# A mixture of softmaxes on one core: stores placed earlier in ScalarE's order, a buffer wait moved to ScalarE, an earlier prior, and a coarser last load

## The chip, the cores and the metric

One NeuronCore of a Trainium2 chip runs the kernel. The metric is the device time of one execution in microseconds (us); medians of several runs are quoted. The profile's span, from the first to the last instruction, is about 1.8 us shorter than the time.

## The reference

```python
prior_probs = softmax(prior, axis=-1)            # [32, 128, 4]
softmax     = softmax(logits, axis=-1)           # [32, 128, 4, 4096], fp32
mixture     = np.sum(prior_probs[..., None] * softmax, axis=2)   # [32, 128, 4096]
```

268.4 MB of logits are read once and 67.1 MB of result written once. Each row (b, s) has four heads of 4096 logits.

## The kernel before

The 4096 rows are cut into 32 units (U) of 128 rows. A unit is loaded to one of two buffers (8.4 MB). ScalarE takes four exponentials with their sums, VectorE takes the reciprocals of the sums, GpSimd multiplies them by the prior, and VectorE adds the four weighted heads into one of two output buffers, which is then stored (2.1 MB).

```python
def load(u):
    if u == 0 or u >= U - 3:
        cuts = (0, 2, 3, 4) if u == U - 1 else (0, 2, 4)
    else:
        cuts = (0, H)
    for h, to in zip(cuts, cuts[1:]):
        ld = nc.sync.dma_start(out=ltile[:, u % 2, h:to], in_=lg[u // J, u % J, :, h:to, :])
        if u >= 2:
            only(ld, adds[u - 2, 0] if h == 0 else exps[u - 2, to - 1])   # all it waits for
        ...
# for each unit u:
free = (stores[u - 2],) if bufd and u >= 2 else ()     # output buffer is free again
m = H if u < U - 4 else 2                              # heads per coefficient step
for h in range(H):
    late = h == H - 1 and 4 <= u < U - 3
    if h == H - 1 and 0 < u < U - 3:
        store(u - 1, obuf[:, (u - 1) % 2], nc.scalar)  # on ScalarE's queue, waits for the last add of u-1
    exp(h, *((stores[u - 4],) if late else ()))
    if (h + 1) % m: continue
    g = h + 1 - m
    mul = weigh(g, m, *(free if g == 0 else ()))       # VectorE reciprocal, then GpSimd product
    for k in range(g, h + 1):
        n = 2 if u == U - 1 and k == H - 1 else 1      # last add of all: two halves,
        for c in range(n):                             # each stored as it is ready
            add(k, mul, c * V // n, (c + 1) * V // n)
            ...
if u + 2 < U: load(u + 2)
# stores of units 28 to 31 are issued on SP's queue, behind the loads
```

A small function that runs at the end of the build moves the very first load ahead of the opening barrier.

The softmax here doesn't subtract the row's maximum and nothing guards it: scores larger than these inputs give would overflow.

## Time and profile before

| | before |
|---|---|
| time, median | 780.93 us |
| span | 779.3 us |
| VectorE, ScalarE busy | 67%, 60% |
| DMA rate over the span | 431 GB/s |

The page also follows the chain of work that ended last. It gives the share of the span by what the chain passed through:

```profile
DMA 64%; ACT 27%; DVE 6%; issue 2%; POOL 0%; DVEq 0%; POOLq 0%
```

For the kernel before it runs mostly through loads.

### The profile page before, as it was taken

The numbers are of one execution on the slowest core, as the hardware profiler recorded it, in microseconds if no ns is written. First come the engines' busy times: TensorE is split into PE (matmuls) and PEld (weight loads), VectorE is DVE, ScalarE is ACT, GpSimd is POOL, SyncE is SP. The second block draws the span as 40 slices with busy tenths as digits, with TensorE's granted clock in tenths as the row PEclk, the third lists the DMA queues.
The fourth block names the chain that finished last, engine by engine and source line by source line (L and its number), as shares of the span: only waits on it lengthen the run. The fifth ranks groups of instructions, "written<-read, shape, count | busy, mean of one in ns | idle before, by whom it ended". The sixth has DMA issues, their size and how long they took to land.

```text
span 779.3 us, 654 instructions
## 1 busy us (share of the span) xinstructions
DVE 521.0 (67%) x174; ACT 466.7 (60%) x258; POOL 8.3 (1%) x41
## 2 busy tenths in 40 slices
DVE  4447875558755587555775557855578655689886
ACT  4476555775457755577555675546765567657782
POOL 0000000000000000000000000000000000000000
DMA  9999999999999999999999999999999999999998
GB/s 407 457 417 401 470 407 434 428 461 428 405 467 403 458 420 433 442 443 418 431 454 407 454 408 467 420 415 447 432 442 417 463 399 463 410 427 433 434 429 377
DMA packets 10117, 335.66 MB, mean 431 GB/s; under 512 B 1136, under 2 KB 1136, under 8 KB 1152
## 3 DMA queue, kind: packets, MB, share of 16 engines
q1 hardware_dynamic: 6048, 276.83, 82.3%
q10 hardware_dynamic: 4064, 58.79, 17.6%
q14 instruction: 5, 0.04, 0.0%
HBM read 268.50 MB, written 67.11 MB: 431 GB/s over the span
## 4 chain that ended last, share of the span: by engine, by line
DMA 64%; ACT 27%; DVE 6%; issue 2%; POOL 0%; DVEq 0%; POOLq 0%
DMA ltile<-in_logits_dram 62%; ACT ebuf L159 19%; ACT ltile L159 8%; DVE obuf L177 5%; DMA out_dram<-obuf 2%; DVE ltile L183 1%; POOL coeff L170 0%; DVE rden L168 0%; DVEq L240 0%; POOLq L240 0%; POOLq L170 0%
## 5 line engine op out<-in xcount | busy, mean ns | idle before, releaser
L183 DVE SCALAR_TENSOR_TENSOR obuf<-ebuf,coeff,obuf 128x4096 f32<-128x4096 f32 x90 | 403.6, 4484 | 3.8 <-POOL coeff L170 0.6
L159 ACT ACTIVATE ebuf<-ltile 128x4096 f32<-128x4096 f32 x90 | 322.9, 3589 | 7.4 <-DMA ltile<-in_logits_dram 7.4
L159 ACT ACTIVATE ltile<-ltile 128x4096 f32<-128x4096 f32 x38 | 137.3, 3614 | 280.6 <-DMA ltile<-in_logits_dram 280.6
L168 DVE RECIPROCAL rden<-dsum 128x4 f32<-128x4 f32 (+1 forms) x36 | 6.3, 175 | 227.9 <-ACT ebuf L159 225.1
L177 DVE TENSOR_SCALAR obuf<-ltile,coeff 128x4096 f32<-128x4096 f32 x30 | 70.6, 2353 | 10.2 <-POOL coeff L170 10.2
L183 DVE SCALAR_TENSOR_TENSOR ltile<-ltile,coeff 128x4096 f32<-128x4096 f32 (+1 forms) x7 | 27.0, 3875 | 0.8 <-POOL coeff L170 0.6
L159 ACT ACTIVATION_READ_ACCUMULATOR ebuf<-ltile 128x1 f32 x90 | 16.8, 186 | 0.0
L170 POOL TENSOR_TENSOR coeff<-rden,pp 128x4 f32<-128x4 f32 (+1 forms) x36 | 7.2, 200 | 755.3 <-DVE rden L168 745.4
L159 ACT ACTIVATION_READ_ACCUMULATOR ltile<-ltile 128x1 f32 x38 | 7.1, 186 | 0.0
L139 DVE TENSOR_REDUCE pmax<-pr 16x256 f32<-16x1024 f32 x1 | 1.2, 1208 | 7.8 <-DMA pr<-in_prior_dram 7.8
L141 ACT ACTIVATE pr<-pr 16x1024 f32<-16x1024 f32 x1 | 1.1, 1055 | 7.8 <-DVE pr L140 7.8
L177 DVE TENSOR_SCALAR ltile<-ltile,coeff 128x4096 f32<-128x4096 f32 x2 | 4.7, 2354 | 0.6 <-POOL coeff L170 0.6
L144 DVE TENSOR_TENSOR pn<-pr,pmax 16x1024 f32<-16x1024 f32 x1 | 1.9, 1939 | 0.1
L141 ACT ACT_TABLE_LOAD x1 | 1.3, 1283 | 1.2 <-PEq L229 1.2
L142 DVE TENSOR_REDUCE pmax<-pr 16x256 f32<-16x1024 f32 x1 | 1.2, 1207 | 1.1 <-ACT pr L141 1.1
L149 DVE STREAM_TRANSPOSE pp<-pn 32x256 f32<-32x256 f32 x4 | 1.7, 435 | 0.1
L143 DVE RECIPROCAL pmax<-pmax 16x256 f32<-16x256 f32 x1 | 1.7, 1741 | 0.0
L140 DVE TENSOR_TENSOR pr<-pr,pmax 16x1024 f32<-16x1024 f32 x1 | 1.2, 1211 | 0.0
L138 POOL MEMSET pn<- 32x1024 f32 x1 | 0.9, 941 | 0.3 <-POOLq L229 0.3
L229 POOL MEMSET const-bfloat16-1.0<- 128x1 bf16 x1 | 0.1, 106 | 0.0
L229 POOL MEMSET const-uint8-127<- 128x1 uint8 x1 | 0.1, 106 | 0.0
L229 POOL MEMSET const-float32-0.0<- 128x1 f32 x1 | 0.1, 103 | 0.2 <-issue 0.2
(1 smaller groups left out, 0.1 us busy)
## 6 DMA issues: line engine op xcount, KB each, us to landing
out_dram<-obuf ACTq DMA_DIRECT2D x28, 2048.0 KB, 29.4
ltile<-in_logits_dram SPq DMA_DIRECT2D x7, 4096.0 KB, 26.1
ltile<-in_logits_dram SPq DMA_DIRECT2D x2, 2048.0 KB, 30.9
out_dram<-obuf SPq DMA_DIRECT2D x2, 2048.0 KB, 33.9
out_dram<-ltile SPq DMA_DIRECT2D x1, 2048.0 KB, 17.2
out_dram<-ltile SPq DMA_DIRECT2D x2, 1024.0 KB, 4.8
ltile<-in_logits_dram SPq DMA_DIRECT2D x28, 30.9
pr<-in_prior_dram ACTq DMA_DIRECT2D x1, 64.0 KB, 7.0
```

What stands on the lines that cost most here:

```text
L139: nc.vector.reduce_max(pmax, pr, axis=AX.X)
L140: nc.vector.tensor_sub(pr, pr, pmax.unsqueeze(2).to_broadcast([G, R, H]))
L141: nc.scalar.activation(pr, pr, AF.Exp)
L142: nc.vector.reduce_sum(pmax, pr, axis=AX.X)
L143: nc.vector.reciprocal(pmax, pmax)
L144: nc.vector.tensor_mul(pn[0:G].rearrange("g h r -> g r h"), pr, pmax.unsqueeze(2).to_broadcast([G, R, H]))
L149: nc.vector.transpose(pp[32 * t : 32 * (t + 1)], pq[:, :, :, 32 * t : 32 * (t + 1)])
L159: ex = nc.scalar.activation(es[h], lt[:, h], AF.Exp, accum_out=dsum[:, u, h : h + 1])
L168: rc = nc.vector.reciprocal(rden[:, u, h : h + n], dsum[:, u, h : h + n])
L170: mul = nc.gpsimd.tensor_mul(coeff[:, u, h : h + n], rden[:, u, h : h + n], ppu[:, h : h + n])
L177: st = nc.vector.tensor_scalar(out=acc[:, lo:hi], in0=es[h][:, lo:hi], scalar1=coeff[:, u, h : h + 1], scalar2=None, op0=ALU.mult,)
L183: st = nc.vector.scalar_tensor_tensor(out=acc[:, lo:hi], in0=es[h][:, lo:hi], scalar=coeff[:, u, h : h + 1], in1=acc[:, lo:hi], op0=ALU.mu ...
```

## The change

The intent, as the change's own words have it: stores ahead of the third exponential (instead of the fourth), the wait for the free output buffer on ScalarE instead of GpSimd, the prior's load also ahead of the opening barrier, and the last unit in two pieces instead of three. The core of the diff:

```diff
-            cuts = (0, 2, 3, 4) if u == U - 1 else (0, 2, 4)
+            cuts = (0, 2, 4)
...
             for h in range(H):
-                late = h == H - 1 and 4 <= u < U - 3
-                if h == H - 1 and 0 < u < U - 3:
+                if h == 2 and 0 < u < U - 3:
                     store(u - 1, obuf[:, (u - 1) % 2], nc.scalar)
-                exp(h, *((stores[u - 4],) if late else ()))
+                exp(h, *(free if m == H and h == H - 1 else ()))
...
-                mul = weigh(g, m, *(free if g == 0 else ()))
+                mul = weigh(g, m, *(free if m < H and g == 0 else ()))
```

The function at the end of the build (cut here) now moves the first DMA of ScalarE, the prior, as well as that of SP.

More of the change, by code (lines that the diff above doesn't have):

```diff
@@ L11, with early_transfers, of @@
 AX = mybir.AxisListType
-def early_first_load(nc):
+def early_transfers(nc):
     blocks = nc.main_func.blocks
-    first = next(
-        (b, i)
-        for b in blocks[1:]
-        for i in b.instructions
-        if i.engine == mybir.EngineType.SP and i.opcode == "DMACopy"
-    )
-    block, ins = first
-    assert not ins.sync_info.on_wait
-    block.instructions.remove(ins)
-    at = next(
-        n
-        for n, i in enumerate(blocks[0].instructions)
-        if i.engine == mybir.EngineType.SP and i.opcode == "Drain"
-    )
-    blocks[0].instructions.insert(at, ins)
+    def of(block, engine, opcode):
+        return next(
+            (i for i in block.instructions if i.engine == engine and i.opcode == opcode), None
+        )
+    for engine in (mybir.EngineType.SP, mybir.EngineType.Activation):
+        body = next(b for b in blocks[1:] if of(b, engine, "DMACopy"))
+        ins = of(body, engine, "DMACopy")
+        assert not ins.sync_info.on_wait
+        body.instructions.remove(ins)
+        drain = of(blocks[0], engine, "Drain")
+        blocks[0].instructions.insert(blocks[0].instructions.index(drain), ins)
 @with_exitstack
@@ L46 @@
     nc = tc.nc
-    nc.at_finalize(early_first_load)
+    nc.at_finalize(early_transfers)
     B, S, H, V = logits.shape
```

## The prediction

> **What bounds the kernel now.** I read the page of the kernel before first, for who is busy:
>
> ```profile
> DVE 521.0 (67%) x174; ACT 466.7 (60%) x258; POOL 8.3 (1%) x41
> ...
> DMA  9999999999999999999999999999999999999998
> ...
> HBM read 268.50 MB, written 67.11 MB: 431 GB/s over the span
> ```
>
> No compute engine is over 67%; the DMA engines are at 90% or more in 39 of 40 slices. A digit of 9 could still hide gaps, so the second view is busy time in stretches (the last two columns are DMA share and GB/s):
>
> ```profile
> 1.00:772.00 771.00, 519.61 (x174) 466.74 (x258) 7.92 (x37) 1.00 1.00 433
> 772.00:777.00 5.00, 1.42 (x1) 0.00 (x0) 0.00 (x0) 1.00 1.00 413
> 777.00:779.30 2.30, 0.00 (x0) 0.00 (x0) 0.00 (x0) 1.00 0.08 32
> ```
>
> From 1.0 to 777 us the sixteen DMA engines are never free. 335.6 MB at 433 GB/s are 775 us of the 779.3. So the middle of the kernel is worth exactly nothing to a change that moves no bytes, unless it starves the queue; only the first microsecond and the last seven can change. The third view is the timeline of one steady unit (start, duration, engine, operation):
>
> ```profile
> 379.04 3.62 ACT L159 ACTIVATE ltile<-ltile 128x4096 f32<-128x4096 f32 x1 [9.67 <-DMA ltile<-in_logits_dram]
> ...
> 385.83 0.34 ACTq L113 DMA_DIRECT2D out_dram<-obuf  x1
> ...
> 386.25 3.56 ACT L159 ACTIVATE ebuf<-ltile 128x4096 f32<-128x4096 f32 x1
> ...
> 389.85 3.60 ACT L159 ACTIVATE ebuf<-ltile 128x4096 f32<-128x4096 f32 x1
> ...
> 396.45 0.33 SPq L100 DMA_DIRECT2D ltile<-in_logits_dram  x1
> 396.46 13.53 DVE L183 SCALAR_TENSOR_TENSOR obuf<-ebuf,coeff,obuf 128x4096 f32<-128x4096 f32 x3
> 403.21 3.62 ACT L159 ACTIVATE ltile<-ltile 128x4096 f32<-128x4096 f32 x1 [9.67 <-DMA ltile<-in_logits_dram]
> ...
> 410.01 0.34 ACTq L113 DMA_DIRECT2D out_dram<-obuf  x1
> ```
>
> A unit starts every 24.17 us (403.21 - 379.04), which is its 10.49 MB at 434 GB/s. ScalarE idles 9.67 us per unit waiting for its load. The load issued at 396.45 (unit 17) cannot begin to move until the one before it (unit 16) has landed, about 402.8, just ahead of its exponential at 403.21: some 6 us of lead. That lead is the number to watch. Last, the end of the timeline, units 30 and 31:
>
> ```profile
> 739.50 3.62 ACT L159 ACTIVATE ltile<-ltile 128x4096 f32<-128x4096 f32 x1 [2.41 <-DMA ltile<-in_logits_dram]
> ...
> 749.22 3.62 ACT L159 ACTIVATE ltile<-ltile 128x4096 f32<-128x4096 f32 x1 [2.41 <-DMA ltile<-in_logits_dram]
> ...
> 756.43 3.60 ACT L159 ACTIVATE ltile<-ltile 128x4096 f32<-128x4096 f32 x1
> ...
> 764.29 9.13 DVE L183 SCALAR_TENSOR_TENSOR ltile<-ltile,coeff 128x4096 f32<-128x4096 f32 x3 [0.31 <-POOL coeff L170]
> ```
>
> The halves of units 30 and 31 arrive 9.72 us apart (739.50 to 749.22). The third exponential of unit 31, at 756.43, shows no wait: its data, cut as a quarter of its own, had come.
>
> **What the Trainium skill says.** (1) "DMA: Bandwidth & Descriptors", section "Where 436 GB/s comes from": sixteen ports give 435.2 GB/s. The trace agrees: 433 to 434 GB/s in full stretches, so the rate has no room left. (2) The same page, "Queues, rings and completion order": each DMA engine takes turns between its queues packet by packet. The trace agrees in kind: a 2 MB store takes 29.4 us (median) to land beside a load, far over the 4.9 us that 2.1 MB take at 434 GB/s, because it shares each turn with the loads' larger rows. (3) "Perfetto Trace Analysis", section "Sequencer Loop": an engine's sequencer takes instructions in order, so what stands behind a waiting DMA issue waits too. The line at 385.83 agrees: the store issues the moment its last add ends (VectorE's run before it ended at 385.8), with the third exponential already handed on.
>
> **The change part by part.**
>
> *Store ahead of the third exponential.* No instruction is added; the order on ScalarE becomes exp, exp, store, exp, exp. The store waits for the last add of the unit before. In the steady state that add ends at 409.99, and the third exponential ran at 410.43 anyway. With the store in front it starts at 410.01 + 0.34 + some hundredths, so about the same. The store itself is issued when the add ends, before and after: nothing gained. It does close a loop: third exponential (386.25) to the end of that unit's adds and the store issue (410.01) is 23.76 us, plus 0.34 for the issue, 24.10 us, plus the dispatch, against a DMA period of 24.17. The loop just fits. In units 2 and 3, whose adds end late (store issues at 72.7 and 95.6), the exponential slips by 1.3 to 1.9 us, and that slip then dies away only slowly.
>
> *Tile wait on ScalarE.* The wait for the store of two units back moves from GpSimd's small product (418.00 in the unit that starts at 403.21) to the fourth exponential (414.02). That store was issued at 385.83; with 29.4 us to landing it is down at 415.2, plus some 0.4 us for the wait to be seen. So the fourth exponential is held for 1.2 to 1.7 us in every unit, where before the wait was over when GpSimd came to it. Slips of the two kinds overlap; they do not add. So the exponentials, the first weighted product and the next load's issue come 1.3 to 2 us later, 26 times. Of the load's lead of 6 us at least 4 remain, and a load needs about 1 us from issue to first bytes (first load: issue at 0.00, DMA busy from 1.0). Cost on the path: 0.
>
> *Prior issued ahead of the opening barrier.* It is issued at about 0.1 instead of 0.79 us. It landed at 7.8; its chain ended with the transposes at 18.2, and the first product that needs it ran at 29.98, after unit 0's last exponential. 0.7 us less of 11.7 us of slack: 0.
>
> *Last unit in two halves.* One of 71 transfers goes, worth about 0 at this rate. But the third exponential must now wait for the whole second half: 749.22 + 9.72 = 758.94 instead of 756.43, so 2.5 us later. The fourth follows at once (it stood at 760.03). The last reciprocal, product and adds all slip by 2.5 us: the last adds start at 766.8 instead of 764.3 and end at 775.9 instead of 773.4.
>
> What of this reaches the end? Ahead of unit 31's stores, the SP queue holds the three stores of units 28 to 30. Behind the last load (landed 758.5, the exponential's wait less some 0.45) they take 3 x 4.86 = 14.6 us, to 773.1 on the latest engines, and unit 31's two half stores 2 x 2.43, to 778.0. Before, the halves were issued at 771.2 and 773.5, in time to queue, so DMA set the end. Now the first half is issued at 773.6 and moves from about 774.5: the engines stand idle for 1.3 to 2.5 us. The second is issued at 775.9, moves from 776.9, is done at 779.3 to 779.4. End: +1.3 to 1.4 us of the 2.5; the rest was queueing.
>
> Sum: 0 + 0 + 0 + 1.35, so 780.93 + 1.35 = 782.3 us.
>
> **The rivals.**
> *A. The loop on ScalarE becomes the bound.* If the dispatch behind the store costs 0.2 us instead of hundredths, the loop is 24.30 us, 0.13 over the DMA period; over 25 units the slip grows by 3.2 us, to about 5, and eats the load's lead. For it: 24.10 against 24.17 is a thin margin. Against: the table load behind the prior's issue followed within 0.03 us (issue 0.79 + 0.39, load at 1.21). It would make 783 to 786 us.
> *B. The end is hidden, or the front gains.* If the second half comes earlier, or the moved prior frees the start, the time stays at 780.5 to 781.2. Against: 9.72 us between halves is steady three times over.
> *C. The whole 2.5 us reach the end*, if the half stores were not queued behind others: 783.4. Against: DMA share 1.00 up to 777 us.
>
> **Range and chances.** Centre 782.3 us. Below, 780.8 is B; above, C and a mild A reach 785. To be 2% off either way takes 15.6 us. A gain of that size is excluded by 775 us of transfers at the ceiling. A loss would need rival A at four times its size. Faster 0.003, same 0.987, slower 0.01.
>
> **What would show it.** In the changed profile: the period of units stays 24.17 us and the DMA share 1.00 up to about 772 us (else A). The fourth exponential waits for a store, 1 to 2 us in most units, and GpSimd no longer does but once or twice near the end. In unit 31 the third exponential waits for its load until about 758.9, the last adds end near 775.9, and a DMA gap of 1 to 2.5 us opens near 773. The span is near 780.7. If the span is 779.3 or less, the step about the last unit was wrong; if the period is over 24.2, the step about the loop was.

## The result, and the profile after

The changed kernel takes 783.14 us (783.01 to 783.27, 6 runs), the kernel before 780.94 us in the same rounds: 2.2 us or 0.28% slower, ratio 1.0028 with a 95% interval of 1.0015 to 1.0041. The span grew by the same 2.2 us, from 779.3 to 781.5.

Busy time by stretches, the changed kernel (the last two columns are DMA share and GB/s):

```profile
1.00:772.00 771.00, 517.12 (x173) 469.89 (x258) 8.13 (x37) 1.00 1.00 433
772.00:777.00 5.00, 3.99 (x2) 0.00 (x0) 0.00 (x0) 1.00 0.53 216
777.00:781.50 4.50, 0.00 (x0) 0.00 (x0) 0.00 (x0) 1.00 0.57 235
```

Up to 772 us the transfers do not differ: 433 GB/s, as before. Then, from 772 to 777 us, the DMA share falls to 0.53, where the kernel before had 1.00 (its line is in the prediction). All but some 0.1 us of the loss arises at the end: unit 31's first exponential starts at 749.34, where it started at 749.22 before.

The end of the timeline shows why (start, duration, engine, line, operation):

```profile
749.34 3.62 ACT L157 ACTIVATE ltile<-ltile 128x4096 f32<-128x4096 f32 x1 [2.41 <-DMA ltile<-in_logits_dram]
...
759.04 3.62 ACT L157 ACTIVATE ltile<-ltile 128x4096 f32<-128x4096 f32 x1 [2.39 <-DMA ltile<-in_logits_dram]
...
766.86 9.14 DVE L181 SCALAR_TENSOR_TENSOR ltile<-ltile,coeff 128x4096 f32<-128x4096 f32 x3 [0.31 <-POOL coeff L168]
773.76 2.60 SPq L111 DMA_DIRECT2D out_dram<-ltile  x2
```

The third exponential of unit 31 now waits 2.39 us for its load, where it ran at 756.43 without a wait. The last adds start at 766.86 instead of 764.29, and the first half store is issued at 773.76. In the kernel before, the same view has the half stores here:

```profile
771.19 2.60 SPq L113 DMA_DIRECT2D out_dram<-ltile  x2
```

The DMA view from 771 to 781.5 us, in 40 slices of 0.26 us (a packet counts in the slice in which it starts, so the first digits are too low), first of the kernel before:

```profile
DMA  4976599999899989899998831100000000000000
```

and of the changed kernel:

```profile
DMA  5911110000000886999977999886999930000000
```

The row of zeros, 772.6 to 774.4 us, is the gap: the queue is empty and the results are still being added. By the packets' own times in the trace, the DMA engines end their earlier stores between 771.8 and 773.16, and the half store starts on them from 774.59.

In the middle, one unit of the changed kernel:

```profile
387.13 0.34 ACTq L111 DMA_DIRECT2D out_dram<-obuf  x1
387.52 3.59 ACT L157 ACTIVATE ebuf<-ltile 128x4096 f32<-128x4096 f32 x1 [1.30 <-DVE obuf L181]
...
411.30 0.34 ACTq L111 DMA_DIRECT2D out_dram<-obuf  x1
411.68 3.59 ACT L157 ACTIVATE ebuf<-ltile 128x4096 f32<-128x4096 f32 x1 [1.29 <-DVE obuf L181]
```

The third exponential now stands behind the store issue and so waits 1.3 us for VectorE's adds. From one third exponential to the next are 24.16 us, the loop that the prediction worked out. The store, though moved ahead in the order, is issued later than before (411.30 against 410.01 us), because the adds that it waits for have slipped too. And the chain that ended last reads:

```profile
DVE 55%; ACT 25%; DMA 15%; issue 2%; ACTq 1%; POOL 1%; DVEq 0%; SPq 0%; POOLq 0%
```

Taken alone this line would say that the kernel has become bound by VectorE. The stretches say that it has not: 433 GB/s throughout. The two paths differ by about a hundredth of a microsecond per unit, and the chain follows whichever ended last.

### The profile page after: what moved, and what is told of

Read it like the earlier page. It is cut to its first block, busy times and chain, and to the rows that moved or that the text cites. A ratio compares the mean times of both kernels' runs of the same rounds, so it can differ in the third digit from the quotient of the medians.

```text
span 781.5 us, 626 instructions
## 1 busy us (share of the span) xinstructions
DVE 521.1 (67%) x174; ACT 470.0 (60%) x258; POOL 8.4 (1%) x41
## 4 chain that ended last, share of the span: by engine, by line
DVE 55%; ACT 25%; DMA 15%; issue 2%; ACTq 1%; POOL 1%; DVEq 0%; SPq 0%; POOLq 0%
DVE obuf L181 45%; ACT ebuf L157 24%; DMA ltile<-in_logits_dram 9%; DVE obuf L175 8%; DMA out_dram<-obuf 6%; ACT ltile L157 1%; ACTq L111 1%; DVE ltile L181 1%; POOL coeff L168 1%; DVE rden L166 1%; DVEq L239 0%; SPq L98 0%; POOLq L239 0%; POOLq L168 0%
## 6 DMA issues: line engine op xcount, KB each, us to landing
ltile<-in_logits_dram SPq DMA_DIRECT2D x28, 29.5
```

## The experiments

Theory: the coarser last load carries the whole loss, and the three other parts are hidden under the transfers. Rival: the late exponentials of the middle cost something too. A third question is how much of a delay at the end stays hidden.

### One part alone, and the change without it

The kernel before with two pieces for the last unit:

```diff
-            cuts = (0, 2, 3, 4) if u == U - 1 else (0, 2, 4)
+            cuts = (0, 2, 4)
```

> The kernel before with one part of the change alone: last unit loaded in two halves instead of a half and two quarters. Theory (the end carries the whole loss): third exponential of unit 31 waits until about 759.0 us, last adds start near 766.8, DMA idle near 772 to 774.5; time 783.1 us, as the full change. Rival (the slipped exponentials in the middle cost something too): clearly under 783, say 782.

Measured: 783.09 us (783.06 to 783.11) against 780.91, ratio 1.0027 (1.0015 to 1.0040). The last adds start at 766.66. Its third exponential of unit 31 and its half stores:

```profile
758.84 3.62 ACT L159 ACTIVATE ltile<-ltile 128x4096 f32<-128x4096 f32 x1 [2.40 <-DMA ltile<-in_logits_dram]
...
773.56 2.60 SPq L113 DMA_DIRECT2D out_dram<-ltile  x2
```

This part alone is as slow as the whole change.

The changed kernel with that line put back:

> The changed kernel with only this part undone: last unit in a half and two quarters again, the other three parts kept. Theory: 780.9 us, the time of the kernel before, with the exponentials of the middle still 1.2 to 1.9 us late. Rival (the middle costs): 781.5 or more.

Measured: 780.97 us against 780.91, ratio 1.0000 (0.9987 to 1.0012), with the third exponentials still 1.2 to 2.5 us late. So the three other parts together, the earlier prior among them, cost and gain nothing that can be seen here (the interval is about 1 us wide either way).

### Dose: the last unit in one piece, and in four

```diff
+            cuts = (0, 4) if u == U - 1 else (0, 2, 4)     # last_one; the piece also waits for exps[u - 2, 3]
+            cuts = (0, 1, 2, 3, 4) if u == U - 1 else ...  # last_four
```

> The kernel before with the last unit loaded in one piece, a larger dose of the same: all four exponentials wait for the end of the load at about 758.96, the last adds start at 758.96 + 4 x 3.61 + 0.5 = 773.9, 7.0 us later than in the changed kernel, with nothing left to hide it. Theory: 783.1 + 7.0 = 790.2 us. Rival (the end hides part of any delay behind the queue of stores): under 789.

Measured: 790.28 us, ratio 1.0119 (1.0105 to 1.0133), last adds from 773.82. The arithmetic from the load's arrival to the end holds to a tenth.

> The kernel before with the last unit in four quarters, a dose in the other direction: the first two exponentials may start earlier, but the third still follows the fourth quarter's neighbours and the end is the DMA queue. Theory: 780.9 us, no gain. Rival (ScalarE's chain sets the end of the kernel before): up to 2 us faster.

Measured: 780.85 us, ratio 0.9999 (0.9985 to 1.0012). Finer than the kernel before brings nothing. The half stores are issued 0.41 us earlier (770.78 against 771.19), and neither the span (779.2) nor the time is shorter by that: an earlier issue buys nothing while earlier stores still fill the queue. The fourth exponential does wait for the last quarter (1.18 us), which it did not in the kernel before.

### The two parts of the middle, each alone

```diff
-                if h == H - 1 and 0 < u < U - 3:       # store_only
+                if h == 2 and 0 < u < U - 3:
```

> The kernel before with one part alone: the store ahead of the third exponential. Theory: 780.9 us; third exponentials slip by 1.3 to 1.9 us in the early units and the slip dies away by hundredths of a microsecond a unit, the period stays 24.17, DMA share 1.00. Rival (the loop store issue to store issue is over the DMA period): the slip grows and the time is over 782.

Measured: 781.01 us against 780.94, ratio 1.0000. The slip of the third exponential (its start after the end of the second) is 1.4 us in unit 2, 2.2 at most, and 1.0 in unit 27: it dies away, as the theory has it.

```diff
-                exp(h, *((stores[u - 4],) if late else ()))   # wait_only
+                exp(h, *(free if m == H and h == H - 1 else ()))
```

with the second argument of `weigh` changed as in the diff above.

> The kernel before with one part alone: the wait for the store of two units back on ScalarE's fourth exponential. Theory of the prediction: the fourth exponential waits 1.2 to 1.7 us for the store in most units; time 780.9. Rival: the wait is nearly always over, as in the changed kernel, where it shows 0.2 us once.

Measured: 781.10 us, ratio 1.0003 (0.9988 to 1.0017). The waits, who for whom, total, times and longest, of this kernel:

```profile
ACT ebuf L159 <- DMA out_dram<-obuf: 29.5, 26, 1.3
```

and of the whole change:

```profile
ACT ebuf L157 <- DVE obuf L181: 35.6, 26, 2.2
...
ACT ebuf L157 <- DMA out_dram<-obuf: 0.2, 1, 0.2
```

Alone, the fourth exponential waits 29.5 / 26 = 1.13 us for a store in every unit, just under the 1.2 to 1.7 that the prediction had worked out. In the whole change the third exponential already waits 1.15 us or more in 26 of 27 units, and by the time the fourth is due the store has landed: one wait covers the other. In unit 21 the third waits only 0.8 us, and that is the one unit whose fourth still waits, 0.2 us, for its store. A wait that is gone from the view was not removed; another one stands in front of it.

### Is the loop on ScalarE and VectorE really at its limit?

Redundant reciprocals, about 0.21 us each, lengthen the loop of the changed kernel without touching a transfer:

```diff
                 only(rc, exps[u, h + n - 1])
+                for _ in range(1):                     # 3 in loop3_after
+                    rc = nc.vector.reciprocal(rden[:, u, h : h + n], dsum[:, u, h : h + n])
+                    only(rc, exps[u, h + n - 1])
```

> The changed kernel with one redundant reciprocal of 128x4 (about 0.19 us with its gap, up to 0.26) added on VectorE ahead of each unit's coefficients, so inside the loop from the third exponential to the store issue. Theory: the loop had 0.01 us to spare, so it becomes 24.36 to 24.42 us and the period of units passes to it: slip grows 0.2 us a unit over 26 units, about 5 us, of which the load's lead of some 4 us hides most; time 783 to 786, and the period in the last third above 24.3 only once the lead is used up. Rival (not on any loop): 783.1 us, slip not growing.

> The same with three redundant reciprocals: loop 24.17 + 0.6 to 0.75 = 24.8 to 24.9 us. Theory: slip grows by 0.6 to 0.7 us a unit, the lead of the loads (about 4 us) is gone after some 6 units, then the units come every 24.8 us: 20 units x 0.65 = 13 us more, 796 us, DMA share below 1. Rival (the middle is bound by transfers whatever ScalarE does): 783.5 us.

Measured: 787.09 us (ratio 1.0077) and 798.76 us (ratio 1.0227; its runs spread from 797.48 to 799.75). The third exponentials come 24.375 us apart with one reciprocal and 24.80 with three, in every unit but one (there 0.3 us more). With one, 26 x (24.375 - 24.165) = 5.5 us are added to the loop and 4.0 reach the time; with three, 26 x 0.635 = 16.5 and 15.6 by the medians, 14.2 by the profiled execution. So the loop is real, it is full, and the loads' lead hid only some 1 to 2 us, not the 4 that was expected of it. The expected times, 783 to 786 and 796, were both somewhat low for this reason. The expectation that the DMA share would drop below 1 was wrong outright. Stretches of the kernel with three reciprocals:

```profile
200.00:400.00 200.00, 132.15 (x64) 118.52 (x67) 1.61 (x8) 1.00 1.00 421
400.00:600.00 200.00, 132.16 (x64) 118.51 (x65) 1.61 (x8) 1.00 1.00 424
```

The share stays 1.00 while the rate falls from 433 to 421 GB/s. In the trace the packets of 64 KB that usually take 2.42 us take up to 3.47 us here, and it is the last of a load's eight on each DMA engine that is long. So the lateness of the loads shows here as long packets, not as idle time. Why a packet is drawn out, no run here shows.

### How much of a delay at the end is hidden?

The kernel before with four or eight redundant reciprocals ahead of the last unit's last coefficients:

```diff
+                for _ in range(4 if (u, h) == (U - 1, 2) else 0):   # 8 in tail8
+                    rc = nc.vector.reciprocal(rden[:, u, h : h + n], dsum[:, u, h : h + n])
+                    only(rc, exps[u, h + n - 1])
```

> The kernel before with four redundant reciprocals (about 0.21 us each, from the loop experiment) ahead of the last unit's second pair of coefficients, so its last adds and half stores come 0.84 us later. The prediction's account: 1.1 to 1.2 us of a delay lie behind the queue of stores, so 780.9 us. Account from the two traces: late DMA engines are free at 773.1 and hide 0.7 us, the closing wait costs up to 0.3 us more once all engines end together: 781.1 to 781.3.

> The same with eight, 1.68 us later. The prediction's account: 1.68 - 1.15, so +0.5: 781.4 us. Account from the traces: first half store moves from 773.7 or 773.8, two halves of 2.58 us each end at 779.0 instead of 778.0, and 0.3 at the close: +1.2 to 1.3, 782.2 us.

Measured: 781.62 us, ratio 1.0009 (0.9997 to 1.0022), and 782.86 us, ratio 1.0025 (1.0011 to 1.0038). Both accounts were too low on the times. The profiles show more, since the issue of the first half store can be read there (one execution each):

| kernel | first half store issued | later by | span | longer by | hidden |
|---|---|---|---|---|---|
| before | 771.19 | | 779.3 | | |
| tail4 | 771.86 | 0.67 | 779.8 | 0.5 | 0.2 |
| tail8 | 772.77 | 1.58 | 780.7 | 1.4 | 0.2 |
| last_two | 773.56 | 2.37 | 781.3 | 2.0 | 0.4 |
| changed kernel | 773.76 | 2.57 | 781.5 | 2.2 | 0.4 |
| last_one | 780.72 | 9.53 | 788.5 | 9.2 | 0.3 |

The end follows that issue almost one for one from the first half microsecond on. At most 0.4 us of any delay is hidden, not 1.1 to 1.2.

The packets in the traces show what this is made of. In the kernel before, eleven of the sixteen DMA engines end their last store by 777.23 us and the latest at 778.01, so there is some 0.8 us of room. In the five other kernels of the table fifteen engines end by 777.89, 778.76, 779.56, 779.76 and 786.69. Counted from 778.01, that is in each case 0.8 us less than the delay of the issue: so much the queue does hide. Two things give part of it back. The sixteenth engine ends later, by 0.5 to 0.6 us in tail4 and tail8 and by 0.15 or less in the others. And the close, from the last store packet to the end of the span, grows from 1.27 us to 1.4 in tail4 and tail8, 1.6 in last_two and the changed kernel, and 1.8 in last_one. For the changed kernel: 2.57 - 0.82 + 0.13 + 0.32 = 2.20 us. Why the close grows is not shown. One thing goes with it: an 8 KB packet of the kind that the DMA view calls "instruction" starts right behind the last store packet in the changed kernel (779.90), last_two and both loop kernels, with closes of 1.56 to 1.59, and before it in nine others, with 1.19 to 1.38; in last_one it comes 1.5 us later, with 1.79. No run moves that packet alone.

In the spans, the account from the traces is close for both (0.2 to 0.4 and 1.2 to 1.3 expected, 0.5 and 1.4 measured).

### Smaller last stores

```diff
-                    n = 2 if u == U - 1 and k == H - 1 else 1
+                    n = 4 if u == U - 1 and k == H - 1 else 1
```

> The changed kernel with the last product added and stored in four pieces of 1024 columns instead of two of 2048. Theory (the end is set by the last adds, with the DMA engines idle before them): the last piece is issued near 776.1, moves from 776.9 and takes 1.3 us: done at 778.3 instead of 779.9, so about 781.6 us. Rival (the end is set by the stores' transfer time): 783.1 or more, as smaller rows move no faster.

> The kernel before with the same four pieces. Theory (its end is the DMA queue, never empty): no gain, 780.9 us within 0.3. Rival (its end too is set by the last adds): 780 or less.

Measured: 782.64 us, ratio 1.0022, and 781.32 us, ratio 1.0006 (0.9993 to 1.0018). On the changed kernel the span fell from 781.5 to 780.4, by 1.1 of the 1.5 us expected (0.24 of it because the last adds started that much earlier, at 766.62), but the time by only 0.5 us; on the kernel before the span is 779.2, unchanged, and the time 0.4 higher. In these two runs, and in tail8, every execution is 2.1 to 2.2 us longer than its span, in the other runs 1.74 to 1.84. What lies in those 0.35 us outside the span is open. What the runs settle is where each end is set: smaller pieces help the kernel whose queue is empty (its DMA share from 772 to 777 us rises from 0.53 to 0.77) and do nothing for the one whose queue is full (0.99).

No version that I ran beats the kernel before. last_four, after_three and store_only tie with it, and its transfers already run at the ceiling from 1 to 777 us.

## Why the prediction was right

- *What bounds the kernel.* Right. The middle was worth nothing: after_three, with all parts but one, takes 780.97 us.
- *Store ahead of the third exponential.* Right in all its numbers: slips of 1.3 to 2.3 us (0.9 in unit 21), dying away up to there, loop of 24.16 us where 24.10 plus dispatch was worked out. Rival A did not come, but by a margin of only about 0.01 us per unit; loop1_after shows that 0.2 more would have made it the result.
- *Tile wait on ScalarE.* The wait exists as worked out (wait_only: 1.13 us in each unit) and costs nothing. That it would be seen in most units of the changed kernel was wrong: the slip in front of it hides it. The load's lead was put at 4 us to spare; by the loop experiments a slip beyond some 3 us already costs (an estimate: the 1.3 us of slip in the middle of the changed kernel and the 1 to 2 us that were hidden). The changed kernel stays under that with 2.3.
- *Prior.* It landed at 5.35 instead of 7.81 us, a larger step than the 0.7 expected, and the first coefficients came at 29.93 instead of 29.98. Not run alone; after_three bounds it together with two other parts.
- *Last unit in two halves.* The mechanism and the first half of its arithmetic were right: third exponential 759.04 (758.9 predicted), last adds 766.86 (766.8), a DMA gap near 773, with the engines idle for some 1.4 to 2.9 us (1.3 to 2.5 predicted). One term was mis-sized, "End: +1.3 to 1.4 us of the 2.5; the rest was queueing". It came to 2.2, and rival C, which lets the whole 2.5 through, was the nearer (783.4 against 783.14; the sum gave 782.3). The queue hid 0.8 us of the delay instead of 1.1 to 1.2, and some 0.4 us came on top that the working did not have: 0.1 from one late engine and 0.3 in the close. The working put the end of the transfers at 779.3 to 779.4; the trace has the last packet of the store at 779.9. The first half started to move at 774.59 rather than 774.5, and the two halves together took up to 5.3 us on an engine rather than the 4.86 of the average rate (their packets of 8 KB took 0.31 us at best, eight of them 2.47, and some up to 0.48). The close of the kernel after the last packet took 1.6 us instead of 1.3. And the DMA share of 1.00 that was held against rival C was read too broadly: in the trace twelve of the sixteen DMA engines had ended their earlier stores by 772.3 us, and the half store began to move at 772.02, so they were at the edge of running empty. Only the latest, at 773.1, had a queue of a microsecond.

The measured time lies inside the range because the range had been drawn upward for C. The sum itself was 0.8 us low, so the hit owes more to the width of the range than to the working of the end.

## What to carry to other kernels

When transfers fill the whole span, read what can still change from the two ends: ask what is the last thing to arrive, and how much work stands between its arrival and the last store; a finer last load and a finer last store shorten exactly that, but only until the queue of earlier stores sets the end (last_four and before_n4 gained nothing). In the middle, changes of order cost nothing only as long as the loops they close stay under the transfer period, so work out the loop before moving a waiting instruction ahead of a compute instruction on the same engine. And check a DMA share of 1.00 against GB/s.

## What the Trainium skill lacked or had wrong

- No page that I used says that the busy share of the DMA engines can stay at 1.00 while they are fed too late: 421 to 424 GB/s at 1.00 in loop3_after, against 433 to 434 GB/s at 1.00 in the kernel before. "Perfetto Trace Analysis", section "Identifying the Most-Contended Engine", does say to judge DMA by its throughput instead of by occupancy, but because there are sixteen engines; stretched packets are a further reason.
- "DMA: Bandwidth & Descriptors", section "Latency and other measured facts", gives about 0.6 us to the first byte of a DMA issued from SP. Here the half store took 0.83 us with the queue empty (issued 773.76, first packet 774.59), and 0.83 to 0.84 in tail4, tail8, last_two and last_one. No page says what lead keeps a queue full: in loop3_after loads were issued some 2.7 us before the previous unit's first exponential (506.27 against 508.96) and the rate fell; in the changed kernel 5.3 us (397.73 against 403.08) lost nothing.
- No page tells that the chain of work that ended last can turn over without any effect on the time: from 64% DMA to 55% VectorE, when two paths differ by about 0.01 us in 24.17 per unit.
